# The opening of a hybrid GDN/MLA encoder block on one core: x issued ahead of the vectors, the first modulation slice in four transfers, its high part in halves on two engines, and the norm spread ahead of the first products

## The chip, the cores and the metric

The kernel runs on one core of a Trainium2 chip. The metric is the device time of one execution in microseconds, taken as the median of several runs. Engines are called as the profile calls them: PE (TensorE, its weight loads apart as PEld), DVE (VectorE), ACT (ScalarE), POOL (GpSimd) and SP (SyncE, which here issues all loads).

## The reference, cut to what matters

One layer of a streaming encoder: a macaron SwiGLU half-step, a token mixer (gated DeltaNet beside latent attention), and a second SwiGLU half-step. Each is fed by an adaptive RMSNorm whose shift, scale and gate come from one small vector `c`. The change sits almost wholly in the first of the three modulations and the first columns of the first SwiGLU product.

```python
D_MODEL = 1024; SEQ = 512; D_FF = 2816; N_MOD = 9

def _modulate(x, shift, scale):
    return _rms(x) * (1.0 + scale[:, None, :]) + shift[:, None, :]

sc = jax.nn.silu(c)
mod = sc @ w_ada[l] + b_ada[l]
sh1, s1, g1, sh2, s2, g2, sh3, s3, g3 = jnp.split(mod, N_MOD, axis=-1)
h = _modulate(x, sh1, s1)
x = x + 0.5 * g1[:, None, :] * _swiglu(h, ffn1_w_in[l], ffn1_w_out[l])
...
```

`x` is 512 tokens by 1024, `w_ada` is 1024 by 9216, `ffn1_w_in` is 1024 by 5632, all float32.

## The kernel before, in words

**Precision.** Each large product is computed from float32 operands that are split into a high part (a cast to the matmul type, on ACT) and a low part (the rest, a subtraction on DVE). `mm3` (L451 to L455) then issues three products: high by high (L453), activations' low part (L454), weights' low part (L455). So each weight tile `wr` becomes `wh` and `wl`, and each tile of the modulated activations `h` becomes `hh` and `hl`.

**The opening** is `setup` (L465) and `phase0` (L484). `setup` issues loads on SP in the order of the code: `c` and `b_ada` as 80 short rows into one tile `vecs`, then `x` as four tiles `xt` of 128 tokens (512 KB each). `phase0` then issues the columns of `w_ada` that give shift and scale of the first 128 model columns ("slice 0", two transfers `ar` of 512 KB, `phase0_slice`, L603), the first 128 rows of the SwiGLU weights for six output blocks (`wr`, 384 KB, `phase0_weights`), the same two for the second 128 columns, and then pairs of slices in eight transfers `ar` of 256 KB each (`phase0_pair`). All transfers go through one queue. Each carries one of eight DMA semaphores in turn, and a semaphore takes one transfer at a time, so SP issues transfer n only when transfer n-8 has landed.

What the engines do until the first product:

- PE transposes `vecs` (L496); ACT makes `sc` = silu(c) from it (L498) and DVE keeps the transposed biases `vT` (L500).
- ACT squares and sums each `xt` (L513); DVE turns the sums into `ve` (L781), POOL takes the power -1/2 (L209), which gives the norm's factor `ry` for each token.
- PE transposes `xt` in eight groups of four blocks (`raw`, L507) and DVE copies each group to `xT` (L508). Seven groups come first, the eighth after the first modulation.
- DVE scales the first 128 columns of x by `ry` (`xn`, L538) and makes `dg`, the factors on a diagonal (L655).
- PE multiplies `sc` with slice 0 in 16 passes (`phase0_cols`, L632), ACT copies the result out (`sg`, L635), PE folds it to two columns (`columns`, L525), DVE adds the biases in two instructions (shift L526, scale L527).
- PE transposes `xn` into one PSUM tile (L547), DVE copies that out (L549), and ACT makes the high part `hh` of the first 128 rows of h from it (L552); DVE makes `m` and the low part (L553, L554). ACT casts the first weights (L544), DVE makes their low part (L556).

**The loop** over the eight 128-row slices of h (`kt`, 0 to 7; L560 on) accumulates six PSUM tiles `pu`. At `kt` = 0 it issues the six high-by-high products (L569), then the spread of the norm's factors over all partitions (a product of `dg` with ones, L663, copied to `rb` by ACT, L571), then for every kt: at the first of six output blocks (`j` = 0) the 16 passes for slice kt+1 (`phase0_cols`), at `j` = 1 `columns` and the modulation of slice kt+1 (`modulated`, L688, L690, L677), and between these the split of the next weights (`weights`, L223 and L224). For kt+1 = 5 and 7 (`SUMMED`) the 16 passes are replaced by eight weighted sums (ACT L641 for the first, DVE L643 for seven) that a table, `STEPS`, hangs on stages kt = 2 and 3, and 4 and 5; there `columns` stands at `j` = 2.

**What sets the order.** All of `phase0` is recorded under `in_order`: each engine runs its instructions in the order in which the code issues them. PSUM tiles from `aux` come from a ring of five buffers, so each takes the place of the fifth before it and waits for that one's readers. What comes behind `phase0` is ordered by a scheduler, and is nearly the same in both kernels. In `gates` (far later, in the mixer) one small copy of `gdn_a_log` was free to move to an early place on DVE.

Of the kernel before, what the change touches and what calls it, by code (L numbers as in the profile page):

```python
# [31 lines left out]
STEPS = {2: (5, range(4)), 3: (5, range(4, 8)), 4: (7, range(4)), 5: (7, range(4, 8))}  # L32
# [60 lines left out]
class Block:  # L93
# [390 lines left out]
    def phase0(self):  # L484
# [10 lines left out]
        pv = self.aux()  # L495
        nc.tensor.transpose(pv[:, :80], self.vecs[:80, :], self.ident[:80, :80])  # L496
        self.sc = self.const([P, 8], s="sc")
        nc.scalar.activation(self.sc, pv[:, 72:80], AF.Silu)  # L498
        self.vT = self.const([P, 72], s="vT")
        nc.vector.tensor_copy(self.vT, pv[:, :72])  # L500
# [3 lines left out]
        def raw(b, j):  # L504
            pt = self.aux()
            for t in range(4):
                nc.tensor.transpose(pt[:, t * P:(t + 1) * P], self.xtok[b][:, (4 * j + t) * P:(4 * j + t + 1) * P], self.ident)  # L507
            nc.vector.tensor_copy(xall[:, 4 * j:4 * j + 4, b * P:(b + 1) * P], pt.rearrange("p (t c) -> p t c", t=4))  # L508

        tiles = [(b, j) for b in range(NB) for j in range(2)]  # L510
# [8 lines left out]
        self.c1, self.c2 = self.const([P, KT], s="sh"), self.const([P, KT], s="s1")  # L519
        self.new_h()  # L520

        def columns(kt, sg, pg, ones):
            k = slice(kt, kt + 1)
            for m in range(2):
                nc.tensor.matmul(pg[:, 256 + m:257 + m], sg[:, m * P:m * P + P], ones, start=True, stop=True)  # L525
            nc.vector.tensor_tensor(out=self.c1[:, k], in0=pg[:, 256:257], in1=self.vT[:, k], op=ALU.add)  # L526
            nc.vector.scalar_tensor_tensor(out=self.c2[:, k], in0=pg[:, 257:258], scalar=1.0, in1=self.vT[:, 8 + kt:9 + kt],  # L527
                                           op0=ALU.add, op1=ALU.add)
# [17 lines left out]
        for b in range(NB):  # L546
            nc.tensor.transpose(pt[:, b * P:(b + 1) * P], xn[:, b * P:(b + 1) * P], self.ident)  # L547
# [1669 lines left out]
```

## Time and profile before

| | us |
|---|---|
| runs shown: median (lowest to highest of 3) | 1040.31 (1040.15 to 1041.21) |
| the profiled execution, own time | 1040.34 |
| its span, first to last instruction | 1038.6 |
| PE busy in the span | 1022.6 (98%) |
| DVE busy | 752.9 (72%) |
| ACT busy | 498.3 (48%) |
| first product of the SwiGLU on PE starts at | 16.03 |
| granted PE clock | 1.000 |

The profiled execution's own time is 1.74 us over its span and 0.03 us over the median of the runs. Times in the views are microseconds from the start of the span. In a row of the timeline the first number is the start, the second the duration, "x4" counts merged instructions, and the bracket tells how long the engine had been idle and what ended that. "SPq" rows are the issue of a transfer, not its run. In the table of stretches each engine has its busy time in that stretch, then come the granted PE clock, the DMA engines' share (over 1 where packets overlap) and their rate in GB/s.

### The profile page before, as it was taken

The numbers are of one execution on the slowest core, as the hardware profiler recorded it, in microseconds if no ns is written. First come the engines' busy times: TensorE is split into PE (matmuls) and PEld (weight loads), VectorE is DVE, ScalarE is ACT, GpSimd is POOL, SyncE is SP. The second block draws the span as 40 slices with busy tenths as digits, with TensorE's granted clock in tenths as the row PEclk, the third lists the DMA queues.
The fourth block names the chain that finished last, engine by engine and source line by source line (L and its number), as shares of the span: only waits on it lengthen the run. The fifth ranks groups of instructions, "written<-read, shape, count | busy, mean of one in ns | idle before, by whom it ended". The sixth has DMA issues, their size and how long they took to land.

```text
span 1038.6 us, 16766 instructions
## 1 busy us (share of the span) xinstructions
PE 1022.6 (98%) x6601; PEld 906.7 (87%) x6601; DVE 752.9 (72%) x1327; ACT 498.3 (48%) x910; POOL 29.7 (3%) x74
## 2 busy tenths in 40 slices
PE   6999999999999999999999999999999999999998
PEld 5788899999887898888788779998999999987888
DVE  5789788887787747868787467787888888783221
ACT  4452455556322235478864455374555555631211
POOL 0000000001100000000000001100000000000000
PEclk9999999999999999999999999999999999999999
DMA  9978234244688745211232021113333334473311
GB/s 331 321 229 257 70 94 122 84 120 128 204 292 293 240 115 145 62 42 41 62 80 68 22 82 41 42 31 100 95 99 105 109 96 121 117 270 105 111 48 42
DMA packets 201501, 130.77 MB, mean 126 GB/s; under 512 B 14017, under 2 KB 186062, under 8 KB 201422
## 3 DMA queue, kind: packets, MB, share of 16 engines
q1 hardware_dynamic: 201422, 129.69, 41.0%
q8 instruction: 52, 0.85, 0.3%
q14 instruction: 27, 0.22, 0.1%
HBM read 127.18 MB, written 2.49 MB: 125 GB/s over the span
## 4 chain that ended last, share of the span: by engine, by line
PE 93%; DVE 3%; issue 2%; DMA 1%; SPq 0%; POOL 0%; ACT 0%; POOLq 0%
PE pa L453 17%; PE pa L454 17%; PE pa L455 17%; PE pa L341 17%; PE pb L341 12%; PE pb L1942 1%; PE pb L453 1%; PE pb L455 1%; PE pb L454 1%; PE pb L1922 1%; DMA ar<-in_w_ada 1%; PE pb L1537 1%; PE pb L632 1%; PE pb L1489 0%; PE pb L1924 0%
## 5 line engine op out<-in xcount | busy, mean ns | idle before, releaser
L223 ACT CAST wh<-wr 128x1024 fp32r<-128x1024 f32 (+1 forms) x104 | 103.7, 1002 | 196.4 <-PE pa L454 171.7
L224 DVE TENSOR_TENSOR wl<-wr,wh 128x1024 fp32r<-128x1024 f32 (+1 forms) x104 | 120.5, 1163 | 79.8 <-ACT wh L223 77.8
L453 PE MATMUL pa<-ah,wh 128*128 128x512 f32 (+1 forms) x396 | 146.5, 370 | 0.0
L454 PE MATMUL pa<-al,wh 128*128 128x512 f32 (+1 forms) x396 | 145.0, 366 | 0.0
L455 PE MATMUL pa<-ah,wl 128*128 128x512 f32 (+1 forms) x396 | 144.9, 366 | 0.0
L257 DVE TENSOR_TENSOR wl<-wr,wh 128x1024 fp32r<-128x1024 f32 x90 | 110.0, 1223 | 44.4 <-ACT wh L261 44.4
L453 PE MATMUL pa<-hh,wh 128*128 128x512 f32 (+1 forms) x357 | 136.9, 383 | 0.0
L455 PE MATMUL pa<-hh,wl 128*128 128x512 f32 (+1 forms) x357 | 135.4, 379 | 0.0
L454 PE MATMUL pa<-hl,wh 128*128 128x512 f32 (+1 forms) x357 | 135.3, 379 | 0.0
L261 ACT CAST wh<-wr 128x1024 fp32r<-128x1024 f32 x90 | 91.8, 1052 | 3.7 <-PE pa L454 2.7
L453 PEld LDWEIGHTS pa<-ah,wh 128*128 128x128 f32 x396 | 74.7, 189 | 14.5 <-ACT wh L223 2.5
L455 PEld LDWEIGHTS pa<-ah,wl 128*128 128x128 f32 x396 | 74.7, 189 | 12.1
L454 PEld LDWEIGHTS pa<-al,wh 128*128 128x128 f32 x396 | 74.7, 189 | 11.7
L813 DVE SCALAR_TENSOR_TENSOR aa<-ar,sc,aa 128x512 f32<-128x512 f32 x98 | 73.4, 750 | 8.1 <-DMA ar<-in_w_ada 6.2
L453 PEld LDWEIGHTS pa<-hh,wh 128*128 128x128 f32 x357 | 67.3, 189 | 13.1 <-ACT th L1264 0.8
L455 PEld LDWEIGHTS pa<-hh,wl 128*128 128x128 f32 x357 | 67.2, 188 | 11.6
L454 PEld LDWEIGHTS pa<-hl,wh 128*128 128x128 f32 x357 | 67.3, 189 | 10.8
L341 PE MATMUL pa<-hh,wh 128*128 128x256 f32 x240 | 68.0, 283 | 0.0
L341 PE MATMUL pa<-th,wh 128*128 128x256 f32 x240 | 67.9, 283 | 0.0
L341 PE MATMUL pa<-tl,wh 128*128 128x256 f32 x240 | 67.9, 283 | 0.0
L341 PE MATMUL pa<-th,wl 128*128 128x256 f32 x240 | 67.9, 283 | 0.0
L341 PE MATMUL pa<-hh,wl 128*128 128x256 f32 x240 | 67.9, 283 | 0.0
(434 smaller groups left out, 2373.1 us busy)
## 6 DMA issues: line engine op xcount, KB each, us to landing
wr<-in_ffn_w_in SPq DMA_DIRECT2D x79, 512.0 KB, 4.9
ar<-in_w_ada SPq DMA_DIRECT2D x104, 256.0 KB, 5.4
wr<-in_ffn_w_out SPq DMA_DIRECT2D x32, 512.0 KB, 4.0
wr<-in_w_in SPq DMA_DIRECT2D x21, 512.0 KB, 3.8
ar<-in_w_ada SPq DMA_DIRECT2D x20, 512.0 KB, 6.4
wr<-in_ffn_w_out SPq DMA_DIRECT2D x16, 384.0 KB, 5.1
wr<-in_w_out SPq DMA_DIRECT2D x8, 512.0 KB, 3.3
wr<-in_ffn_w_in SPq DMA_DIRECT2D x8, 384.0 KB, 5.9
```

The costliest lines, as they stand in the source:

```text
L223: self.nc.scalar.copy(hi, raw)
L224: self.nc.vector.tensor_tensor(out=lo, in0=raw, in1=hi.bitcast(F32), op=ALU.subtract)
L257: sub = lambda out, x, y: nc.vector.tensor_tensor(out=out, in0=x, in1=y, op=ALU.subtract)
L261: nc.scalar.copy(hi[:, :n], raw[:, :n])
L341: nc.tensor.matmul(z, a[:, j, :], b, start=start and j == 0 and i == 0, stop=j == 3 and i == 2, skip_group_check=not start)
L453: mm(out, wh, xh, start=start, stop=False)
L454: mm(out, wh, xl, start=False, stop=False)
L455: mm(out, wl, xh, start=False, stop=stop)
L632: nc.tensor.matmul(pg[32 * q:32 * q + 32, :256], self.sc[:, kc:kc + 1].to_broadcast([P, 32]), a[kc], start=(e == 0), stop=(e == 1), tile_p ...
L813: nc.vector.scalar_tensor_tensor(out=acc, in0=a, scalar=sc, in1=acc, op0=ALU.mult, op1=ALU.add)
L1537: nc.tensor.matmul(pa[:, ps], kh[:, ps], x[:, ps], start=True, stop=True)
L1922: nc.tensor.matmul(ps[:, :n], self.qnT[h][:, ts], self.knT[h][:, :n], start=True, stop=False)
```

## The change

It does seven things, all in the opening but the last:

1. SP issues `x` first, then `c` and `b_ada`.
2. Slice 0 is loaded in four transfers: rows 0 to 767 of `w_ada` for shift and for scale, then rows 768 to 1023 for each.
3. The transpose of `vecs`, `sc` and `vT` move behind the fifth group of x transposes and behind the squares; DVE also makes the biases once as pairs (`cb`), so that `columns` is one DVE instruction for shift and scale together (`c12`).
4. Three of the eight copies to `xT` (groups 5 to 7) go from DVE to ACT, and the eighth group's transposes move ahead of slice 0's passes.
5. `xn` is transposed into two PSUM tiles of 256 tokens. The high part of the first tile of h is made straight from them: the first half on ACT, the second on DVE. The copy to SBUF (L549) is gone.
6. The spread of the norm's factors stands ahead of the first products instead of behind them; the split of the next weights moves behind the modulation at kt = 1 and 2; the sums of slices 5 and 7 are placed by a new table (`ORDER`: before, within and after the modulation), and `columns` stands at `j` = 1 for them too.
7. In `gates` the copy of `gdn_a_log` is tied behind the first instruction there.

```diff
-STEPS = {2: (5, range(4)), 3: (5, range(4, 8)), 4: (7, range(4)), 5: (7, range(4, 8))}
+ORDER = {2: ((), (), ((5, range(3)),)), 3: (((5, range(3, 5)),), ((5, range(5, 6)),), ((5, range(6, 8)),)),
+         4: ((), (), ((7, range(3)),)), 5: (((7, range(3, 5)),), ((7, range(5, 6)),), ((7, range(6, 8)),))}
...
     def setup(self):
-        self.load(self.vecs[72:80, :], ins["c"].rearrange("o (t p) -> (o t) p", p=P))
-        self.load(self.vecs[0:72, :], ins["b_ada"].rearrange("o (t p) -> (o t) p", p=P))
         xd = ins["x"][0]
...
+        self.load(self.vecs[72:80, :], ins["c"].rearrange("o (t p) -> (o t) p", p=P))
+        self.load(self.vecs[0:72, :], ins["b_ada"].rearrange("o (t p) -> (o t) p", p=P))
...
-        for i in range(4):
-            raw(*tiles[i])
+        for i in range(5):
+            raw(i, nc.vector.tensor_copy)
         r = self.rms_cols(v, NB, D)
-        for i in (4, 5, 6):
-            raw(*tiles[i])
+        pv = self.aux()
+        nc.tensor.transpose(pv[:, :80], self.vecs[:80, :], self.ident[:80, :80])
+        nc.scalar.activation(self.sc, pv[:, 72:80], AF.Silu)
+        nc.vector.tensor_copy(self.vT, pv[:, :72])
+        nc.vector.tensor_copy(bias[:, :, 0], self.vT[:, :8])
+        nc.vector.tensor_scalar(out=bias[:, :, 1], in0=self.vT[:, 8:16], scalar1=1.0, scalar2=None, op0=ALU.add)
+        for i in range(5, 8):
+            raw(i, nc.scalar.copy)
...
-            nc.vector.tensor_tensor(out=self.c1[:, k], in0=pg[:, 256:257], in1=self.vT[:, k], op=ALU.add)
-            nc.vector.scalar_tensor_tensor(out=self.c2[:, k], in0=pg[:, 257:258], scalar=1.0, in1=self.vT[:, 8 + kt:9 + kt],
-                                           op0=ALU.add, op1=ALU.add)
+            nc.vector.tensor_tensor(out=c12[:, kt, :], in0=pg[:, 256:258], in1=bias[:, kt, :], op=ALU.add)
...
-        nc.vector.tensor_copy(t, pt)
         columns(0, *cols)
+        pr = self.spread_diag(dg, NB)
...
-        nc.scalar.activation(hh, t, AF.Identity, scale=self.c2[:, 0:1], bias=self.c1[:, 0:1])
-        nc.vector.tensor_scalar(out=m, in0=t, scalar1=self.c2[:, 0:1], scalar2=self.c1[:, 0:1], op0=ALU.mult, op1=ALU.add)
+        nc.scalar.activation(hh[:, l], pts[0], AF.Identity, scale=self.c2[:, 0:1], bias=self.c1[:, 0:1])
+        for out, pt, ts in ((hh, pts[1], u), (m, pts[0], l), (m, pts[1], u)):
+            nc.vector.tensor_scalar(out=out[:, ts], in0=pt, scalar1=self.c2[:, 0:1], scalar2=self.c1[:, 0:1],
+                                    op0=ALU.mult, op1=ALU.add)
...
     def phase0_slice(self, kt):
-        for m in range(2):
-            self.load(a[:, :, m, :], a1[:, m * D + kt * P:m * D + (kt + 1) * P].rearrange("(k p) n -> p k n", p=P))
+        for k0, k1 in ((0, 6), (6, KT)) if kt == 0 else ((0, KT),):
+            for m in range(2):
+                self.load(a[:, k0:k1, m, :], a1[k0 * P:k1 * P, m * D + kt * P:m * D + (kt + 1) * P].rearrange(
+                    "(k p) n -> p k n", p=P))
```

**SP, the first transfers.** Here stand the loads from the start of the program: `vecs` is c and b_ada, `xt` a tile of x, `ar_100` slice 0, `wr` weights, `ar_107` (then `ar_109`) slice 1. Before:

```order
L131 DMA vecs_73<-in_c 8x128
L131 DMA vecs_73<-in_b_ada 72x128
L131 DMA xt_76<-in_x 128x1024
L131 DMA xt_78<-in_x 128x1024
L131 DMA xt_80<-in_x 128x1024
L131 DMA xt_82<-in_x 128x1024
L131 DMA ar_100<-in_w_ada 128x8x128 x2
L131 DMA wr_103<-in_ffn_w_in 128x2x384
L131 DMA ar_107<-in_w_ada 128x8x128 x2
```

The same engine and place in the change:

```order
L132 DMA xt_74<-in_x 128x1024
L132 DMA xt_76<-in_x 128x1024
L132 DMA xt_78<-in_x 128x1024
L132 DMA xt_80<-in_x 128x1024
L132 DMA vecs_73<-in_c 8x128
L132 DMA vecs_73<-in_b_ada 72x128
L132 DMA ar_100<-in_w_ada 128x6x128 x2
L132 DMA ar_100<-in_w_ada 128x2x128 x2
L132 DMA wr_105<-in_ffn_w_in 128x2x384
L132 DMA ar_109<-in_w_ada 128x8x128 x2
```

The two vector loads have moved from the first two places to the fifth and sixth, and slice 0 has become four transfers; everything behind them keeps its order and its sizes.

**PE, from the last x transposes to the first products.** `pb_186` and `pb_248` before are the seventh and eighth group of x transposes, `pb_220` slice 0's passes and their fold, `pb_232` the transposed `xn`, `dg_215` the diagonal of the norm, `pa_254` the first of the six accumulators. Before:

```order
L507 MATMUL pb_186<-ident_84,xt_82 128x128 x4
L632 MATMUL pb_220<-ar_100,sc_132 32x256 x8
L547 MATMUL pb_232<-ident_84,xn_210 128x128 x4
L525 MATMUL pb_220<-sel_136,sg_229 128x1 x2
L507 MATMUL pb_248<-ident_84,xt_82 128x128 x4
L569 MATMUL pa_254<-hh_194,wh_104 128x512
...
L569 MATMUL pb_259<-hh_194,wh_104 128x512
L663 MATMUL pb_271<-dg_215,ones_89 128x512
L632 MATMUL pb_274<-ar_107,sc_132 32x256 x8
```

In the change (`pb_180` is the transposed `vecs`, `pb_186` to `pb_198` the last three groups of x, `pb_242` and `pb_243` the two halves of `xn`):

```order
L521 MATMUL pb_180<-ident_84,vecs_73 128x80
L506 MATMUL pb_186<-ident_84,xt_78 128x128 x4
L506 MATMUL pb_192<-ident_84,xt_80 128x128 x4
L506 MATMUL pb_198<-ident_84,xt_80 128x128 x4
L652 MATMUL pb_230<-ar_100,sc_136 32x256 x8
L552 MATMUL pb_242<-ident_84,xn_220 128x128 x2
L552 MATMUL pb_243<-ident_84,xn_220 128x128 x2
L532 MATMUL pb_230<-sel_132,sg_239 128x1 x2
L683 MATMUL pb_251<-dg_225,ones_89 128x512
L586 MATMUL pa_262<-hh_204,wh_106 128x512
...
L586 MATMUL pb_267<-hh_204,wh_106 128x512
L652 MATMUL pb_278<-ar_109,sc_136 32x256 x8
```

The spread (L663, now L683) has moved from behind the six products to ahead of them, the eighth group of x from behind the fold to ahead of slice 0's passes, and the transpose of `vecs` from the head of PE's program into the groups of x.

**DVE, stages kt = 2 and 3 of the loop.** `hm` is the modulated slice, `hl` its low part, `wl` the next weights' low part, `sg_394` (then `sg_395`) the sum for slice 5. Before, from the end of stage 2's modulation:

```order
L677 SCALAR_TENSOR_TENSOR hl_201<-hm_390,sh_192,hh_200 128x512
L643 SCALAR_TENSOR_TENSOR sg_394<-ar_313,sc_132,sg_394 128x256
L643 SCALAR_TENSOR_TENSOR sg_394<-ar_315,sc_132,sg_394 128x256
L643 SCALAR_TENSOR_TENSOR sg_394<-ar_317,sc_132,sg_394 128x256
L224 TENSOR_TENSOR wl_368<-wr_366,wh_367 128x768
L526 TENSOR_TENSOR sh_192<-pb_436,vT_134 128x1
L527 SCALAR_TENSOR_TENSOR s_193<-pb_436,vT_134 128x1
L688 SCALAR_TENSOR_TENSOR hm_454<-xT_98,s_193,rb_270 128x512
L643 SCALAR_TENSOR_TENSOR sg_394<-ar_319,sc_132,sg_394 128x256
L643 SCALAR_TENSOR_TENSOR sg_394<-ar_321,sc_132,sg_394 128x256
L677 SCALAR_TENSOR_TENSOR hl_203<-hm_454,sh_192,hh_202 128x512
L643 SCALAR_TENSOR_TENSOR sg_394<-ar_323,sc_132,sg_394 128x256
```

The same place in the change:

```order
L541 TENSOR_TENSOR wl_312<-wr_310,wh_311 128x768
L663 SCALAR_TENSOR_TENSOR sg_395<-ar_316,sc_136,sg_395 128x256
L663 SCALAR_TENSOR_TENSOR sg_395<-ar_318,sc_136,sg_395 128x256
L541 TENSOR_TENSOR wl_370<-wr_368,wh_369 128x768
L663 SCALAR_TENSOR_TENSOR sg_395<-ar_320,sc_136,sg_395 128x256
L663 SCALAR_TENSOR_TENSOR sg_395<-ar_322,sc_136,sg_395 128x256
L533 TENSOR_TENSOR c_135<-pb_435,cb_134 128x2
L708 SCALAR_TENSOR_TENSOR hm_455<-xT_98,c_135,rb_260 128x512
L663 SCALAR_TENSOR_TENSOR sg_395<-ar_324,sc_136,sg_395 128x256
L697 SCALAR_TENSOR_TENSOR hl_213<-hm_455,c_135,hh_212 128x512
L663 SCALAR_TENSOR_TENSOR sg_395<-ar_326,sc_136,sg_395 128x256
L663 SCALAR_TENSOR_TENSOR sg_395<-ar_328,sc_136,sg_395 128x256
```

One of the sums has moved from stage 2 into stage 3, two now stand between the weights' low part and the bias instruction, one instead of two between the modulation and its low part, and the bias instructions are one. Stages 4 and 5 change in the same way for slice 7.

More of the change, by code (lines that the diff above doesn't have):

```diff
@@ L569, in phase0 @@
                     nc.tensor.matmul(pu[j], hi[:, j, :], xh, start=True, stop=False)
[L570 to L571 removed]
+            early = ORDER.get(kt, ((), (), ()))
             for j in range(6):
                 if j == 0 and more:
[L574 to L575 removed]
                     if kt + 1 in SUMMED:
@@ L578, in phase0 @@
                     else:
+                        if kt > 2:
+                            high(kt + 1)
                         cols = self.phase0_cols(kt + 1, slices[kt + 1])
-                    if kt in (1, 2):
-                        w = weights(kt + 1)
-                if j == (2 if kt + 1 in SUMMED else 1) and more:
+                    if kt > 2:
+                        if kt + 1 in SUMMED:
+                            high(kt + 1)
+                        low(kt + 1)
+                    for e in early[0]:
+                        steps(*e)
+                if j == 1 and more:
                     columns(kt + 1, *cols)
@@ L585, in phase0 @@
                     next(made)
[L586 to L595 removed]
+                    for e in early[1]:
+                        steps(*e)
+                    drain(made)
+                    if kt < 3:
+                        high(kt + 1)
+                        low(kt + 1)
+                    for e in early[2]:
+                        steps(*e)
                 if kt > 0:
```

74 lines of the change are left out of this document (34 added, 40 removed).

## The prediction, made before the change was run

> **What bounds the kernel now.** I read the busy shares first, then the table of stretches, to see where TensorE stands still.
>
> ```profile
> PE 1022.6 (98%) x6601; PEld 906.7 (87%) x6601; DVE 752.9 (72%) x1327; ACT 498.3 (48%) x910; POOL 29.7 (3%) x74
> 0.00:3.00 3.00, 0.10 (x1) 0.12 (x1) 0.00 (x0) 1.49 (x2) 1.32 (x11) 1.00 0.29 34
> 3.00:6.00 3.00, 0.57 (x3) 0.36 (x4) 0.30 (x2) 0.50 (x2) 0.00 (x0) 1.00 0.87 325
> 6.00:10.00 4.00, 4.00 (x25) 4.00 (x24) 2.77 (x4) 3.65 (x7) 0.00 (x0) 1.00 1.05 381
> 10.00:16.00 6.00, 3.26 (x34) 2.17 (x31) 4.89 (x16) 2.54 (x5) 1.02 (x1) 1.00 1.13 359
> 16.00:24.00 8.00, 7.97 (x56) 4.92 (x56) 4.54 (x8) 2.41 (x4) 0.00 (x0) 1.00 1.09 390
> 23.04:60.00 36.96, 36.96 (x217) 28.25 (x217) 27.02 (x51) 18.76 (x30) 0.00 (x0) 1.00 0.85 284
> 60.00:1000.00 940.00, 935.96 (x6068) 835.98 (x6067) 708.45 (x1241) 463.88 (x856) 27.33 (x62) 1.00 0.40 119
> ```
>
> From 23 to 60 us TensorE has no gap, and from 60 to 1000 it has 4 us of them. So every later microsecond is TensorE's own work, and an opening that ends earlier shifts all of it. The DMA engines' share is full from 6 to 24 us at 359 to 390 GB/s: the opening is a race between one full queue and the small work that needs what it brings.
>
> Next the timeline of the opening, cut to the chain that leads to the first product, and the loads that it needs.
>
> ```profile
> 0.81 0.41 SPq L131 DMA_DIRECT2D vecs<-in_c  x1
> 1.27 0.31 SPq L131 DMA_DIRECT2D vecs<-in_b_ada  x1
> 1.63 1.78 SPq L131 DMA_DIRECT2D xt<-in_x  x4
> 2.90 0.36 PE L496 MATMUL pb<-ident,vecs 80*128 80x80 f32 x1 [2.90 <-DMA vecs<-in_b_ada]
> 3.45 2.21 SPq L131 DMA_DIRECT2D ar<-in_w_ada  x2
> 5.68 1.06 ACT L513 ACTIVATE jk<-xt 128x1024 f32<-128x1024 f32 x1 [2.19 <-DMA xt<-in_x]
> 10.65 0.17 DVE L781 TENSOR_SCALAR ve<-v 128x4 f32<-128x4 f32 x1 [0.67 <-ACT jk L513]
> 10.91 1.02 POOL L209 TENSOR_TENSOR ry<-ve,mhalf 128x4 f32<-128x4 f32 x1 [8.89 <-DVE ve L781]
> 12.53 0.87 DVE L538 TENSOR_SCALAR xn<-xt,ry 128x128 f32<-128x128 f32 x4
> 12.59 1.09 PE L632 MATMUL pb<-ar,sc 128*32 128x256 f32 x16 [2.02 <-DMA ar<-in_w_ada]
> 13.61 0.66 PE L547 MATMUL pb<-ident,xn 128*128 128x128 f32 x4
> 13.75 0.37 ACT L635 COPY sg<-pb 128x256 f32<-128x256 f32 x1 [3.13 <-PE pb L632]
> 14.02 0.84 ACT L544 CAST wh<-wr 128x768 fp32r<-128x768 f32 x1
> 14.18 0.61 PE L525 MATMUL pb<-sel,sg 128*128 128x1 f32 x4
> 14.91 0.15 DVE L526 TENSOR_TENSOR sh<-pb,vT 128x1 f32<-128x1 f32 x1
> 15.16 0.81 ACT L552 ACTIVATE hh<-hm,sh,s 128x512 fp32r<-128x512 f32 x1 [0.30 <-DVE s L527]
> 16.03 0.96 PE L569 MATMUL pa<-hh,wh 128*128 128x512 f32 x3 [0.75 <-ACT hh L552]
> ```
>
> TensorE waits 2.02 us for slice 0; from there each step starts when the one before ends, until the first product at 16.03. The norm's branch is no better: `ry` is ready at 11.93, but `xn` starts at 12.53, since DVE is copying x groups. The chain of waits, which follows the end of the program back to its causes, agrees, and prices three more steps:
>
> ```profile
> 4.15 8.30 DMA ar<-in_w_ada
> 17.68 0.86 PE pb L663 x2
> 23.11 1.02 PE pb L632 x16
> 24.14 0.43 PE pa L453
> ```
>
> Slice 0 lands at 4.15 + 8.30 = 12.45; the spread costs TensorE 0.86; slice 2's 16 passes start at 23.11, and the products of kt = 1 follow at 24.14. One more row tells when the queue has brought slice 2:
>
> ```profile
> 22.93 0.37 SPq L131 DMA_DIRECT2D ar<-in_w_ada  x1
> ```
>
> By the order of loads this is the eighth transfer behind the last one of slices 2 and 3, with the same semaphore, and SP has issued seven since; so it is that landing that lets it go, at about 22.91. In the kernel before it was harmless: the last two of the 16 passes, which alone need it, start at 23.11 + 14/16 of 1.02 = 24.00.
>
> **The change part by part.** *The queue.* x is issued at 0.81 (where `c` was) and not at 1.63: 0.82 us earlier. The 40 KB of vectors now stand in the full queue: 0.11 at 0.36 MB/us. Everything behind them keeps sizes and order, so it lands 0.71 earlier, if the queue stays full. Bounds: 0, if the queue's start-up does not move, to 0.82. I take 0.71, because x is 2 MB at the head of a queue that was filling just then (34, then 325 GB/s). Slice 0 lands at 11.74, its first three quarters at 11.74 - 0.26/0.36 = 11.0.
>
> *Slice 0's passes.* Twelve of 16 need only the first two transfers: 11.15 (a landing is followed 0.14 later, 12.45 to 12.59) to 11.9. The last four take 0.26 behind 11.88, so the passes end near 12.15; before, at 13.68.
>
> *The norm.* Four squares end 0.82 earlier; `ve` at 9.83, `ry` at 11.11. DVE has no x copies left there, only the bias preparation (three small instructions, the nearest row L526 with 0.15), so `xn` runs from 11.2 to 12.1, just before TensorE is free for it at 12.15. The two transposes of 0.66 end at 12.8.
>
> *To the first product.* `sg` 12.2 to 12.6, the fold (0.61) behind the transposes 12.75 to 13.35, one bias instruction instead of two until 13.65. For the high part on ACT no row shows a half tile from PSUM: the nearest are the 128x256 copy `sg` (0.37) and the 128x512 row of L552 (0.81). I take 0.45, nearer to the copy, which has the same size and source. Ahead of it stands the cast of the weights (0.84), which need 384 KB behind slice 0: 11.74 + 0.39/0.36 = 12.8, so 12.85 to 13.7, and the half tile ends near 14.2. DVE's half is done earlier. The spread (0.86) fills TensorE's wait from 13.35 to 14.2. First product: **14.25, 1.78 earlier**. And behind the six products 0.86 of spread is gone, so TensorE reaches slice 2's passes 2.64 earlier, at 20.47. Slice 1 lies between: 1 MB and 384 KB behind slice 0 need 4.0 us at 359 GB/s, so it lands at 15.75, and TensorE asks for it at 14.25 + 1.65 = 15.9. Just in time.
>
> *Slice 2.* Its last transfer lands at 22.91 - 0.71 = 22.2. The passes for the others run ahead; the last two start at 22.34 and not at 24.00. So of 2.64 us gained **1.0 is given back as a wait for the queue, and 1.65 stays.**
>
> *Costed at nothing, with their cover.* That 1.0 us of wait covers anything that makes the first product late by less.
>
> ```profile
> 7.71 0.69 DVE L508 COPY xT<-pb 128x512 f32<-128x512 f32 x1 [0.16 <-PE pb L507]
> 18.58 0.59 ACT L571 COPY rb<-pb 128x512 f32<-128x512 f32 x1 [2.60 <-PE pb L663]
> ```
>
> The three copies on ACT (0.59 to 0.69 each) lie between the squares' end and `sg`, 10.05 to 12.1; each 0.1 over that delays `sg` by as much. The vectors land near 9.1 (4.86 and three more tiles, then 0.11) instead of before 2.9; `sc` then waits for the fourth square on ACT (about 10.05) and is needed at 11.15; behind their transpose on PE stand three x groups, which wait with it. SP issues two transfers more, and the eight-semaphore rule now makes the quarter transfers wait for x tiles 1 and 2 (5.68 - 0.82 = 4.86, and one tile of 0.52 MB at 0.38 MB/us later, 6.2); behind them queue all further loads, but at 6.2 the queue still holds two x tiles and three quarters of slice 0, 1.8 MB or 4.9 us. The copy in `gates` moves 16 bytes a partition. The sum, made against the profiled execution's own 1040.34 (span 1038.6, 0.03 over the median): 1040.34 - 1.65 = **1038.7**.
>
> [...] The stretch at 16 to 24 us carries mostly 256 KB transfers at 390 GB/s, that at 10 to 16 mostly 512 KB ones at 359: in a full queue smaller was not slower. [...]
>
> **The rivals.** *The queue moves further than thought, and TensorE does not wait for slice 2.* Then all 2.64 stay: 1037.7. For it: the first x packets come while the queue is empty. Against it: the queue has been full since 6 us, and it would have to land 1.7 earlier with 0.8 of head start.
>
> *The queue does not move.* If filling it takes until about 4 us whatever is issued first (325 GB/s in 3 to 6), slice 2 lands at 22.91, its last passes start at 23.05: 0.95 earlier, 1039.4.
>
> *DVE becomes the bound in stages 3 and 5 (slower than the forecast, and than before if it grows).*
>
> ```profile
> 29.92 0.50 PE L453 MATMUL pa<-hh,wh 128*128 128x512 f32 x1
> 34.57 1.52 DVE L643 SCALAR_TENSOR_TENSOR sg<-ar,sc,sg 128x256 f32<-128x256 f32 x3
> 35.74 0.50 PE L453 MATMUL pa<-hh,wh 128*128 128x512 f32 x1
> 36.00 0.95 DVE L224 TENSOR_TENSOR wl<-wr,wh 128x768 fp32r<-128x768 f32 x1
> 37.46 0.75 DVE L688 SCALAR_TENSOR_TENSOR hm<-xT,s,rb 128x512 f32<-128x512 f32 x1
> 39.05 0.74 DVE L677 SCALAR_TENSOR_TENSOR hl<-hm,sh,hh 128x512 fp32r<-128x512 f32 x1
> 40.46 0.39 PE L453 MATMUL pa<-hh,wh 128*128 128x512 f32 x1
> ```
>
> Stage 3 lasts 4.72 us on TensorE (35.74 to 40.46). DVE's work in it rises to five sums (0.51 each), 0.95, 0.75, 0.74 and 0.15, in all 5.1, and the fold of slice 5 comes one block (0.69) sooner. If DVE enters the stage without slack, TensorE waits 0.4 + 0.69 = 1.1, and again in stage 5: 1040.9. It decides if DVE ends stage 2 later than TensorE; stage 2 lasts 5.8 us (29.92 to 35.74) and has by the same rows 3.6 of DVE work (0.75, 0.74, 0.95, 0.15 and two sums), so I expect slack.
>
> *The two extra transfers hold up the queue (slower than before).* The vectors' 36 KB took 1.6 us from issue (1.27) to use (2.90). If each extra transfer stopped the queue for as long, slice 2 would land 3.2 later, at 25.4, its last passes start at 25.55 and the kernel ends at 1041.9. It decides from 1.65 us of stop on. Against it: in the stretches above the share stays full over some twenty transfers. [...]
>
> **How the numbers follow.** The forecast has 0.58, with 1038.7. No wait for slice 2: 0.16 (1037.7). A queue that does not move: 0.10 (1039.4). DVE: 0.08 (1040.9). Extra transfers: 0.06 (1041.9). Else 0.02. The range 1037.3 to 1040.2 holds the first three, with half a microsecond for the unknown durations at either end, and leaves out the rest. A measurement of this kernel can tell about 0.2%, 2.1 us, from no change: faster than 1038.2 is the second case and a tenth of the first (0.22), slower than 1042.4 is half of the last rival and the rest (0.05), and 0.73 lies between.
>
> **What would show it.** Right: the first x tile used at about 4.85; slice 0's passes in two parts ending near 12.2; the first product (L586) at 14.25, within 0.5; the spread (L683) ahead of it; about 1 us of TensorE waiting for `ar` within slice 2's passes; the first product of kt = 1 near 22.5; no gap from there to 60. Wrong: no wait at slice 2's passes (second case), that wait with the old landing (third), gaps at `columns` of slices 5 and 7 (DVE), or a DMA share that drops between 9 and 13 us (transfers).

## The result and the profile after

The kernel after takes **1041.93 us** (median of 22 runs, 1041.32 to 1046.0); the kernel before, run beside it, 1040.37 (22 runs, 1039.65 to 1042.99). The ratio is 1.0017, 95% interval 1.0011 to 1.0023: 1.6 us slower, where the prediction had 1.65 us faster. Its range ended at 1040.2. The profiled execution of after took 1041.64 with a span of 1039.8, so 1.30 more than that of before.

The table of stretches first, of the kernel after, for the five stretches in which before was shown:

```profile
0.00:3.00 3.00, 0.00 (x0) 0.00 (x0) 0.16 (x1) 1.49 (x2) 1.31 (x11) 1.00 0.34 81
3.00:6.00 3.00, 1.45 (x7) 1.48 (x8) 0.32 (x1) 1.44 (x3) 0.00 (x0) 1.00 1.01 385
6.00:10.00 4.00, 3.05 (x22) 2.85 (x21) 2.95 (x5) 3.08 (x7) 0.00 (x0) 1.00 1.08 351
10.00:16.00 6.00, 5.00 (x35) 2.91 (x34) 3.25 (x15) 3.47 (x9) 1.02 (x1) 1.00 1.16 302
16.00:24.00 8.00, 7.84 (x52) 4.60 (x51) 4.81 (x8) 2.18 (x4) 0.00 (x0) 1.00 1.08 352
```

Until 6 us the queue did what was predicted: it starts earlier and fills sooner (81 and 385 GB/s, before 34 and 325). Then it falls behind: 351, 302 and 352 GB/s where before had 381, 359 and 390. The DMA engines' share stays over 1 all the while (1.08, 1.16 and 1.08). So the queue never stands empty; each byte takes the engines longer.

Next the timeline of the kernel after, TensorE's rows of the opening, with the first use of x on ACT ahead of them:

```profile
4.44 1.06 ACT L516 ACTIVATE jk<-xt 128x1024 f32<-128x1024 f32 x1 [2.15 <-DMA xt<-in_x]
11.82 1.88 PE L652 MATMUL pb<-ar,sc 128*32 128x256 f32 x16 [0.99 <-DVE xn L545]
13.64 0.66 PE L552 MATMUL pb<-ident,xn 128*128 128x128 f32 x4
14.17 0.60 PE L532 MATMUL pb<-sel,sg 128*128 128x1 f32 x4
14.64 1.11 PE L683 MATMUL pb<-dg,ones 128*128 128x512 f32 x2
15.76 0.93 PE L586 MATMUL pa<-hh,wh 128*128 128x512 f32 x3
...
17.44 1.09 PE L652 MATMUL pb<-ar,sc 128*32 128x256 f32 x16
...
21.97 2.27 PE L652 MATMUL pb<-ar,sc 128*32 128x256 f32 x14
24.99 0.62 PE L652 MATMUL pb<-ar,sc 128*32 128x256 f32 x2 [0.75 <-DMA ar<-in_w_ada]
25.54 0.50 PE L454 MATMUL pa<-hh,wh 128*128 128x512 f32 x1
```

The last three rows are slice 2's passes and the first product of kt = 1. In the kernel before they read:

```profile
23.05 1.09 PE L632 MATMUL pb<-ar,sc 128*32 128x256 f32 x16
24.07 0.50 PE L453 MATMUL pa<-hh,wh 128*128 128x512 f32 x1
```

x is used 1.24 earlier than before (5.68), but the first product starts only 0.27 earlier (16.03), and TensorE's lead of 1.08 at slice 2's passes (21.97, before 23.05) turns into a loss: 16 passes that need 1.02 take until 25.54, waiting for transfer after transfer. The first product of kt = 1 starts 1.47 later than before (24.07). That is the whole loss (1.30 in the executions' own times): from 60 us on TensorE is busy 240.00 of 240.00 us to 300 in both kernels, and then 695.89 to 1000 us here against 695.96. (The bracket at 11.82 names `xn`; but `xn` runs from 11.42 to 12.29. It was the second of slice 0's four transfers, whose last part landed at 11.69.)

Two things were read from single DMA packets and from semaphores. In the opening of before a packet of 512 B took 27 ns, one of 1024 B 46 and one of 1536 B 65, nearly always the same (7826 of 7835 packets from 8 to 26 us); in after 512 B took 32 on average in 8 to 16 us (28 to 33 from one microsecond to the next), 1024 B 51 and 1536 B 79. And the semaphore of each large transfer goes up by one sixteen times (for slice 2's last transfer in before from 22.21 to 22.91); each count is taken here for the landing of one part, on one of the sixteen DMA engines, though the trace doesn't name the engine. The table gives, for the last transfer of slice 2, when the first, the fifteenth and the last part landed, with what followed:

| run | slice 0 last | slice 2 first / 15th / last part | first product of kt = 1 | own time |
|---|---|---|---|---|
| before | 12.45 | 22.21 / 22.80 / 22.91 | 24.07 | 1040.34 |
| before again (e1) | 12.96 | 22.64 / 24.25 / 25.02 | 25.61 | 1041.83 |
| after | 12.55 | 23.34 / 24.28 / 24.95 | 25.54 | 1041.64 |
| e4, tiles at 256 B | 11.72 | 21.39 / 22.93 / 23.17 | 23.76 | 1039.61 |
| e13, e4 again | 11.88 | 21.72 / 23.43 / 23.68 | 24.27 | 1039.89 |
| e5, before at 64 B | 12.94 | 24.09 / 24.64 / 24.68 | 25.27 | 1041.29 |
| e6, after at 128 B | 12.23 | 23.41 / 23.92 / 25.44 | 26.03 | 1041.70 |

The time is the start of that product plus 1015.6 to 1016.3 us in every row: what the opening gains or loses is settled there. These are single executions, and not always typical ones: those of e4 and e5 are among the fastest of their eleven runs (e5's the very fastest), those of e7 and e10 below are the slowest of theirs.

### The profile page after: what moved, and what is told of

Read it like the earlier page. It is cut to its first block, busy times and chain, and to the rows that moved or that the text cites. A ratio compares the mean times of both kernels' runs of the same rounds, so it can differ in the third digit from the quotient of the medians.

```text
span 1039.8 us, 16774 instructions
## 1 busy us (share of the span) xinstructions
PE 1024.5 (99%) x6601; PEld 907.1 (87%) x6601; DVE 751.5 (72%) x1319; ACT 499.2 (48%) x913; POOL 29.6 (3%) x74
## 4 chain that ended last, share of the span: by engine, by line
PE 90%; DVE 3%; DMA 2%; issue 2%; ACT 1%; SPq 1%; POOL 0%; DVEq 0%; ACTq 0%; POOLq 0%
PE pa L454 17%; PE pa L455 17%; PE pa L456 17%; PE pa L342 17%; PE pb L342 12%; SPq L132 1%; PE pb L1962 1%; PE pb L454 1%; PE pb L455 1%; PE pb L456 1%; DMA wr<-in_ffn_w_in 1%; DMA ar<-in_w_ada 1%; PE pb L1942 1%; PE pb L1509 1%; ACT bd L1587 0%
## 5 line engine op out<-in xcount | busy, mean ns | idle before, releaser
L224 ACT CAST wh<-wr 128x1024 fp32r<-128x1024 f32 (+1 forms) x97 | 97.8, 1015 | 197.4 <-PE pa L455 176.0
L225 DVE TENSOR_TENSOR wl<-wr,wh 128x1024 fp32r<-128x1024 f32 (+1 forms) x97 | 113.7, 1178 | 75.9 <-ACT wh L224 74.3
```

The lines of the kernel that those rows point to most:

```text
L224: self.nc.scalar.copy(hi, raw)
L225: self.nc.vector.tensor_tensor(out=lo, in0=raw, in1=hi.bitcast(F32), op=ALU.subtract)
```

## The experiments

Ratios are to the kernel before in runs on the same chip (21 to 33 runs of it each time, medians 1040.36 to 1040.79). The sets ran on three chips (the first and the fourth on one), so times of different sets are compared by the ratios; where medians are compared across sets, the text says so.

**First set: is it the change at all, and which part of the issue order?** Both kernels with no edit, one execution each, then after with the vectors issued first, and after with slice 0 in two transfers:

```diff
 e2     def setup(self):
+        self.load(self.vecs[72:80, :], ins["c"]...)
+        self.load(self.vecs[0:72, :], ins["b_ada"]...)
         xd = ins["x"][0]
 e3     def phase0_slice(self, kt):
-        for k0, k1 in ((0, 6), (6, KT)) if kt == 0 else ((0, KT),):
+        for k0, k1 in ((0, KT),):
```

> The kernel before, unchanged, for its packets beside those of the others on one chip. Theory 1 (the change itself slows the transfers' queue): 359 GB/s from 10 to 16 us and 390 from 16 to 24, as in its first trace, first product near 16.0, products of kt = 1 from 24.1. Rival (the slow queue in the trace of the change belongs to that chip or that execution): 300 to 350 GB/s here as well, and slice 2's passes wait for the queue.

> The changed kernel, unchanged. Theory 1: 300 GB/s from 10 to 16 us and 350 from 16 to 24 once more, products of kt = 1 from 25.5. Rival (chip or execution): a rate that differs from the first trace, with first product and slice 2 moved along with it, and no fixed distance to the kernel before.

> The changed kernel with the loads of c and b_ada ahead of x, as before; all else stays. Theory 1a (the order of issue upsets the queue): the rate is back at 359 and 390 GB/s, slice 0 lands at 12.45 as before, slice 2 at 22.9 and kt = 1 starts 0.95 earlier than before: about 1039.4, 2.5 us faster than the changed kernel. Theory 1b (the four transfers upset the queue): rates stay at 300 and 350, the time at about 1041.9.

> The changed kernel with slice 0 in two transfers of 512 KB, x still first. Theory 1a (the order of issue upsets the queue): rates stay at 300 and 350 GB/s, the time at about 1041.9 or a little more, since all of slice 0's passes wait for its end. Theory 1b (the four transfers upset the queue): rates of 359 and 390, slice 2 lands 0.7 earlier than before, about 1038.7.

The stretch from 10 to 16 us of each, in this order:

```profile
10.00:16.00 6.00, 3.32 (x32) 2.27 (x32) 4.68 (x16) 2.59 (x5) 1.02 (x1) 1.00 1.11 331
```
```profile
10.00:16.00 6.00, 6.00 (x39) 4.22 (x38) 2.75 (x14) 3.90 (x9) 1.03 (x1) 1.00 1.14 305
```
```profile
10.00:16.00 6.00, 4.63 (x33) 2.51 (x31) 3.19 (x16) 3.60 (x9) 1.02 (x1) 1.00 1.15 305
```
```profile
10.00:16.00 6.00, 4.17 (x39) 2.97 (x39) 2.67 (x15) 3.52 (x9) 1.02 (x1) 1.00 1.15 305
```

Three kernels with the change have the same 305 GB/s and packets of 32 and 51 ns on average; before has 27 and 46 ns again, so the longer packets belong to the change and not to the chip. The second run of after took 1042.28 us. And neither edit undid it: e2 1042.81 us, ratio 1.0026 (1.0017 to 1.0035); e3 1041.97, 1.0015 (1.0006 to 1.0023). Both theories on the issue order fell. The second profile of before told something else: nearly all its packets are as short as ever, and yet it moved 331 GB/s and took 1041.83 us, 1.5 more than in the first. Four packets from 14 to 16 us took 0.84 to 1.42 us each. The parts of slice 1's first transfer landed within 1.2 us, those of its second, at that time, within 2.7, and slice 2's last part landed at 25.02. The trace doesn't say which engine had which packet, so that these four delayed those parts is an inference.

**Second set: where the tiles lie.** What remained was something that all kernels with the change share. In the built program of before the SBUF tiles that the opening's loads go to start at a multiple of 256 B in their partition (`ar` of slice 0 at 203776, the first `wr` at 56320); in after each starts 64 B past one (203840, 56384). The cause is in the diff, in words that look like bookkeeping: two small constants of 32 B in a partition (`sh`, `s1`) became two of 64 B (`cb`, `c12`), and everything behind them moved by 64 B. So: the same two kernels, instruction for instruction, with one small constant widened.

```diff
-        self.sel4 = self.const([P, 1], s="sel4")
+        self.sel4 = self.const([P, 49], s="sel4")[:, :1]    (e4, after: 192 B more, tiles back at 256 B)
+        self.sel4 = self.const([P, 17], s="sel4")[:, :1]    (e5, before: 64 B more; e6, after: at 128 B)
```

> The kernel after, instruction for instruction the same, with the small tile sel4 widened from 1 to 49 columns: 192 B more per partition, so that every later SBUF tile (the x tiles, the slices, the weight tiles, the slots) starts at a multiple of 256 B again, as in the kernel before; in the kernel after they start 64 B past one. Theory 2 (the place of the destinations in SBUF slows the queue): packets of 512 and 1024 B back at 27 and 46 ns (after: 31 to 34 and 51), the core's transfers back near 359 GB/s in 10 to 16 us and 390 in 16 to 24 (after: 302 and 352), first product for k-tile 1 at 22.4 to 23.2 us (after: 25.54), median 1038.3 to 1039.3 us. Rival (the slower queue comes from the order or the number of what is issued, in a way that neither vectors first nor two transfers undid): 302 and 352 GB/s and 1041.9 us, as after.

> The kernel before, instruction for instruction the same, with sel4 widened from 1 to 17 columns: 64 B more per partition, so that every later SBUF tile starts 64 B past a multiple of 256 B, as in the kernel after, and nothing else of the change. Theory 2: packets at 31 to 34 and 51 ns, about 302 GB/s in 10 to 16 us and 350 in 16 to 24; the 5.27 MB that before moves from 10 to 24 us then take some 16 us, so slice 2 lands 1.5 to 2.3 us later and the median is 1041.8 to 1042.8 us. Rival: 27 and 46 ns, 359 and 390 GB/s, 1040.4 us.

> The kernel after with sel4 widened to 17 columns: every later SBUF tile starts 128 B past a multiple of 256 B. [...] Theory 2 with steps of 128 B: as on a multiple of 256 B, 27 and 46 ns, 359 and 390 GB/s, 1038.3 to 1039.3 us. If places do not matter: 1041.9 us, and the run on a multiple of 256 B gives that as well.

The stretches 10 to 16 and 16 to 24 us of e4, then of e5, then of e6:

```profile
10.00:16.00 6.00, 5.35 (x36) 3.22 (x35) 3.85 (x16) 3.55 (x7) 1.02 (x1) 1.00 1.12 347
16.00:24.00 8.00, 7.63 (x52) 4.19 (x51) 4.02 (x6) 1.95 (x4) 0.00 (x0) 1.00 1.08 383
```
```profile
10.00:16.00 6.00, 3.82 (x36) 2.74 (x34) 4.69 (x16) 1.97 (x5) 1.02 (x1) 1.00 1.15 305
16.00:24.00 8.00, 7.48 (x49) 4.77 (x52) 4.23 (x9) 2.87 (x5) 0.00 (x0) 1.00 1.10 345
```
```profile
10.00:16.00 6.00, 5.99 (x40) 3.80 (x39) 3.38 (x15) 3.87 (x7) 1.02 (x1) 1.00 1.17 305
16.00:24.00 8.00, 7.14 (x49) 4.25 (x47) 4.49 (x7) 1.87 (x4) 0.00 (x0) 1.00 1.10 352
```

The same instructions have packets of two lengths, and the place of the tiles chooses which. e4 has packets of 27 and 46 ns; e5 and e6 have 32 to 33 and 51 on average. The packet's length is the surer sign: the rate in GB/s also falls when single packets take very long, as in the second profile of before (331 from 10 to 16 us) and in e7 below (303), both with packets of 27 ns. Medians: e5 1043.01, ratio 1.0024 (1.0015 to 1.0033): 64 B of padding alone make the kernel before at least as slow as the change did (1041.8 to 1042.8 was expected). e6 1041.70, 1.0009 (0.9999 to 1.0019): 128 B off costs the packets what 64 B off costs (32 to 33 and 51 ns in both), so Theory 2 with steps of 128 B fell, though its time alone would not tell it from e4's. e4 1040.88 (1039.32 to 1042.02), 1.0001 (0.9992 to 1.0010): the loss against before is gone. But the gain of 1.65 is not there either, and e4 missed what was expected of it (1038.3 to 1039.3); that took two more sets.

That the place does it is shown; how it does it is not. 1536 B packets took longer too, some 76 ns in e5 and e6 against 65 in before, but 4096 B packets, and packets in the emptier queue from 60 us on, took no longer (see the last section).

**Third set: what sets the time once the rate is back?** In e4, TensorE's rows around slice 2 (those of before stand above):

```profile
21.04 1.88 PE L652 MATMUL pb<-ar,sc 128*32 128x256 f32 x14
23.21 0.62 PE L652 MATMUL pb<-ar,sc 128*32 128x256 f32 x2 [0.30 <-DMA ar<-in_w_ada]
23.76 0.50 PE L454 MATMUL pa<-hh,wh 128*128 128x512 f32 x1
```

TensorE is 2.01 us ahead of before at the passes (21.04 against 23.05) and has 0.31 left behind them: it still waits for slice 2, whose last part landed at 23.17. So in e7 (on e4) and e8 (on after) these passes stand two output blocks later, and two more undo one part each of the change, where nothing hides it any longer.

```diff
+            late = 2 if kt == 1 else 0
             for j in range(6):
-                if j == 0 and more:
+                if j == late and more:
...
-                if j == 1 and more:
+                if j == late + 1 and more:
                     columns(kt + 1, *cols)
```

> The kernel after with its tiles at multiples of 256 B (as e4) and one more edit: in k-tile 1 TensorE does slice 2's passes and their column sums two products groups (6 products, 2.06 us) later, so that it goes on with k-tile 1's products in place of waiting for slice 2. Theory A (in the kernel after, and still in e4, the landing of slice 2's last transfer sets the time, and TensorE's lead from the earlier stages is given back there): the first product for k-tile 1 moves from 23.76 us in e4 to about 21.1, the passes then take 1.1 us without a wait, and some 1.3 to 1.7 us are kept: median 1038.9 to 1039.7 us (e4 1040.88). Rival (TensorE isn't what is late there; what follows k-tile 1 waits for something else, such as slice 4 or the modulation, which starts 2 us later): within 0.4 us of e4, 1040.5 to 1041.3 us.

> The kernel after as it is (tiles 64 B past multiples of 256 B) with slice 2's passes two groups of products later, as in e7. Theory A: the wait that the slow queue makes at slice 2 (passes 21.97 to 25.54 us, 2.5 us more than their 1.02) is covered for 2.06 us; what is left is up to 0.5 us there and the later landing of slice 0 (0.7 us against e4), so 1039.6 to 1040.6 us, within 1.2 us of e7, and the packets stay at 33 and 51 ns. Rival: 1041.5 to 1042.3 us, as after.

> e7 with the norm's spread and its copy put back behind k-tile 0's first six products, as in the kernel before: the one term of the prediction that moved work (0.86 us). Prediction's account (the spread lies in a wait for the first products when it is ahead of them, and TensorE's lead counts once nothing waits at slice 2): 0.5 to 0.9 us slower than e7. Rival (the first products then start earlier by nearly as much, since the high part in halves is ready by then): within 0.2 us of e7.

> e7 with slice 0 in two transfers, as in the kernel before: prices the four transfers where no landing of slice 2 hides them. Prediction's account: passes of slice 0 that start when all has landed end some 0.7 us after the landing more (1.09 us of passes, of which 0.41 stay behind the last landing with four transfers): 0.5 to 0.8 us slower than e7. Rival (what follows the passes waits for xn or the weights' high part, not for the passes): within 0.2 us of e7.

| run | median (lowest to highest of 11) | ratio (95%) |
|---|---|---|
| e7 | 1039.33 (1038.67 to 1040.34) | 0.9985 (0.9977 to 0.9994) |
| e8 | 1040.30 (1040.12 to 1041.80) | 0.9996 (0.9987 to 1.0005) |
| e9 | 1039.80 (1039.38 to 1040.54) | 0.9986 (0.9977 to 0.9995) |
| e10 | 1039.24 (1038.79 to 1040.62) | 0.9986 (0.9977 to 0.9995) |

Theory A holds: covering the wait is worth 1.6 us (e7 to e4, by the medians and by the ratios, whose intervals overlap by 0.0002), as predicted, and with the slow queue as much or more (e8 to after, 1.6 by the medians and 2.2 by the ratios, whose intervals lie apart). In the profiled execution of e7 slice 0 landed late (12.51), so that the products of kt = 1 start at 22.76 and not at 21.1; but the passes run without a wait, though slice 2's last part landed only at 24.89. Its passes, then the products of kt = 1 in e8, which run on until the passes, two groups later:

```profile
24.87 1.09 PE L653 MATMUL pb<-ar,sc 128*32 128x256 f32 x16
```
```profile
21.78 0.50 PE L454 MATMUL pa<-hh,wh 128*128 128x512 f32 x1 [0.17 <-ACT wh L537]
22.12 0.40 PE L455 MATMUL pa<-hl,wh 128*128 128x512 f32 x1
22.77 0.50 PE L456 MATMUL pa<-hh,wl 128*128 128x512 f32 x1 [0.26 <-DVE wl L541]
```

Of the two parts, the spread behaves as predicted in the trace of e9. The rows show the wait that it otherwise fills, and slice 1's passes 0.84 later than in e4 (16.49):

```profile
14.92 0.93 PE L583 MATMUL pa<-hh,wh 128*128 128x512 f32 x3 [0.98 <-ACT hh L557]
15.69 0.85 PE L583 MATMUL pb<-hh,wh 128*128 128x512 f32 x3
16.38 1.02 PE L683 MATMUL pb<-dg,ones 128*128 128x512 f32 x2
17.33 1.09 PE L652 MATMUL pb<-ar,sc 128*32 128x256 f32 x16
```

In the time it is 0.47 by the medians and not told from nothing by the ratios (0.9986 and 0.9985). The four transfers are worth nothing that can be measured (e10 is 0.09 under e7), where 0.5 to 0.8 was expected.

**Fourth set: why four transfers gain nothing, what x first is worth, and the late part.**

```diff
 e11    def phase0_cols(self, kt, a):
-        for q in range(4):
-            for e in range(2):
-                kc = 2 * q + e
+        for e in range(2):
+            for q in range(4):
+                kc = q + 4 * e
```

> e7 with the passes dealt to TensorE's four column groups the other way: group q takes rows q and q+4 of the slice's eight, not 2q and 2q+1 (the sums over the eight are the same sums in another order). Theory B (why four transfers were worth nothing in e10): in e4 the last four records of slice 0's 16 passes, all of one column group, start 0.21 us apart (11.86, 12.08, 12.29, 12.51) where 16 over four groups start 0.05 apart, so the quarter that lands last costs 1.03 us, as much as all 16 (1.09) after a single landing. With the last quarter in two groups its two pairs overlap: passes of slice 0 end 0.43 us earlier after the landing, first product 0.3 to 0.45 earlier, median 1038.8 to 1039.1 us (e7 1039.33). Rival (xn or the weights' cast is what the first product waits for): 1039.2 to 1039.5.

> e7 with c and b_ada issued ahead of x, as in the kernel before: prices the earlier issue of x (0.82 us) where neither the slow queue nor the wait at slice 2 hides it. Prediction's account: all landings 0.71 us later, first product 0.6 to 0.8 later, median 1039.9 to 1040.2 us (e7 1039.33). Rival (the queue's start sets the landings whatever is issued first, or the vectors that land late behind x cost as much as x gains): within 0.2 us of e7.

> e4's kernel again, for a second profile. In e4 single packets took up to 1.4 us from 14 to 16 us, their DMA engines stayed behind the others by that much, and slice 2's last sixteenth landed at 23.17 where the other engines had brought theirs by 22.4. Theory C (this belongs to the execution and not to the kernel): other engines or none fall behind this time, slice 2 lands between 22.2 and 23.5 accordingly, and the time goes with it (1038.7 to 1039.1 us without a late engine, 1040 and more with one later than e4's). Rival (it belongs to the kernel's order of transfers): the same delay at the same place and 1039.3 to 1039.8 us.

First e4, slice 0's passes and what follows them; then e11:

```profile
11.14 1.75 PE L652 MATMUL pb<-ar,sc 128*32 128x256 f32 x16 [0.64 <-DMA ar<-in_w_ada]
12.82 0.66 PE L552 MATMUL pb<-ident,xn 128*128 128x128 f32 x4
...
14.93 0.94 PE L586 MATMUL pa<-hh,wh 128*128 128x512 f32 x3
```
```profile
11.20 1.42 PE L653 MATMUL pb<-ar,sc 128*32 128x256 f32 x16
12.55 0.66 PE L552 MATMUL pb<-ident,xn 128*128 128x128 f32 x4
...
14.67 0.94 PE L586 MATMUL pa<-hh,wh 128*128 128x512 f32 x3
```

From slice 0's landing to the transposes of `xn`, which follow the passes, e4 needs 1.10 us (11.72 to 12.82) and e11 0.69 (11.86 to 12.55): 0.41 less, where 0.43 was expected. e10, with slice 0 in two transfers, needs 1.16 (12.32 to 13.48): four transfers dealt as in e4 save 0.06. In e4 the last four records start at 11.86, 12.08, 12.29 and 12.51; in e11 at 11.99, 12.00, 12.21 and 12.24, two side by side. Theory B holds in the traces. The median is **1038.67** (1038.14 to 1039.78), ratio 0.9979 (0.9970 to 0.9988): this version is faster than both kernels, 0.2% under before. From e7 it differs by 0.0006, less than the intervals tell apart, so the 0.41 is not shown in the time.

e12 takes 1039.96 us, 0.9993 (0.9984 to 1.0002): 0.63 over e7 by the medians and 0.8 by the ratios, about what the prediction gave the earlier issue of x (0.71). The two intervals overlap (e7's ends at 0.9994), so this isn't told from nothing either. In its profile slice 0 lands at 12.84 and the first product starts at 16.05, where e4 has 11.72 and 14.93; a part of that is one late part, since the fifteenth part of slice 0 had landed at 12.27.

e13 took 1039.89. Its slow packets are others than e4's (above their usual duration 0.36 us in all from 14 to 15, 0.55 from 16 to 17 and 0.65 from 17 to 18, where e4 had 3.7 us from 14 to 16), its slice 2 landed 0.5 later and its time is 0.28 longer. So size and place of the slow packets go with the execution. But parts were late in this run too, as in every profile but two: the gap from the first to the last part of slice 2 was 0.70 in the first profile of before and 0.59 in e5, and 1.5 to 3.3 us in the other fourteen. Neither theory holds alone. That slow packets held up slice 2's last part is an inference in e4 too: which engine had which packet is not in the trace, and the fifteenth part landed at 22.93. What makes the slow packets stays open; a likely second cause of late parts, which comes too late to matter in those two profiles, stands in the last section.

## Why the prediction was wrong, point by point

- **The step that failed** is "Everything behind them keeps sizes and order, so it lands 0.71 earlier, if the queue stays full." It stayed full and kept sizes and order, and its rate fell all the same, by 8% from 6 to 10 us and by 10 to 16% from there on, since the change's two small constants moved every tile that is loaded by 64 B. Slice 2's first part landed at 23.34 (22.21 before) and its last at 24.95, where the forecast had 22.2; 0.67 of that is the last part alone, which the last section puts down to something else. The prediction read the diff for what it makes the engines do, not for what it does to addresses; its "queue" rivals were about issue and start-up, and no rival had the rate itself change. Shown by e4, e5 and e6: same instructions, other places. In e5, where nothing but the place changed, slice 2's last part landed 1.77 later than in before (24.68). In time, the place is worth 1.0 us by the medians and 1.7 by the ratios (e4 to after) of the 3.2 by which the forecast was missed.
- **That slice 2's landing sets the end** was right, and costlier than thought: 1.0 us was to be given back there, and the lead of 1.08 was lost with 1.47 on top. Shown by e7 and e8.
- **x first** came out as forecast in four of six profiles with x first and the tiles at 256 B: the first part of slice 2 landed at 21.39 to 21.72 in e4, e9, e11 and e13, against 22.21 before (0.71 earlier forecast, 0.49 to 0.82 measured), and slice 0 at 11.71 to 11.88 (11.74 forecast). In e7 and e10, with 13 and 12 slow packets, that part came at 22.17 and 22.16, hardly earlier than before. e12 puts the price at 0.63 by the medians, within the noise.
- **"The last four take 0.26"** was wrong. It took a quarter of the time of 16 passes that overlap over four column groups (in before each record lasts 378 ns and the starts are 0.05 us apart); the last quarter lies in one group and its records follow each other every 0.21 to 0.22 us, 1.03 us in all. Passes that were to end near 12.15 in a queue with before's rate end at 12.89 in e4, and the first product starts at 14.93 and not at 14.25. Shown by the traces of e10 and e11. In e4 itself this cost nothing at the end: TensorE was at slice 2's passes at 21.04, 2.13 ahead of the last landing, so the wait covered it, as the prediction had said of anything late by less than that wait.
- **The landing of a transfer** was taken from the mean rate and from one profile, in which the sixteen parts landed within 0.7 us. The slowest of the sixteen parts counts: in e9 fifteen parts had landed at 22.18, just where the forecast had the whole, and the last at 23.11. The second profile of before shows that it has such executions too. In e4's profiled execution the last part at 23.17 moved the first product of kt = 1 from the forecast 22.5 to 23.76, and it took 1039.61 and not 1038.7. Its eleven runs fall into two groups, 1039.32 to 1039.79 and 1040.88 to 1042.02, and the median is the lowest of the second; no trace of that group was kept, so that its loss comes from late landings too is likely but not shown.
- **The spread ahead** (0.86) fills the wait as forecast; e9's trace has it (0.84), its time only in part. The half tile on ACT took 0.56 (L558, forecast 0.45).
- **The rivals.** No gap at `columns` of slices 5 and 7: all of TensorE's 0.75 us of idle time from 24 to 60 us in after lie ahead of 24.99. Small transfers: the two last pieces of slice 0, 128 KB each, landed 0.35 and 0.37 behind what stood ahead of them in e4, the queue's full rate (128 KB in 0.36 us is 364 GB/s). The rival of extra transfers named the right time, 1041.9, by the wrong cause, which is luck: e3 has two transfers less and the same time. The prediction also took a difference under 2.1 us for one that can't be told from none; with 22 runs of each kernel the interval is 1.2 us wide, and the 1.6 us of loss are clear of it. And its range reaches 0.4 us below and 0.8 above the cases that it holds, not half a microsecond at either end.

## What to carry to other kernels

Before pricing a change, compare the addresses of what the DMA writes: two small constants that grew by 32 B each, allocated ahead of the large tiles, cost this kernel 1.0 to 1.7 us (after, by medians and by ratios) and 2.6 us (the same shift in before), against 1.65 that the change was meant to gain, and 192 B of padding undo it. Ask of a wait for a transfer whether work behind it could go first (e7: three lines, 1.6 us), and expect a landing at its slowest part, not its mean (23.11 against 22.18 for the fifteenth in e9). Ask of a load cut in pieces whether the work on the last piece still fills the engine: here four transfers saved 0.06 us behind the landing with the last four passes in one column group (e4) and 0.41 more with them in two (e11), and that 0.41 is not seen in the time.

## What the runs showed of the hardware that was not expected

- Packets to SBUF tiles that start 64 or 128 B past a multiple of 256 B took mostly 33 on average instead of 27 ns (512 B) and 51 instead of 46 (1024 B) while the queue was full, in all seven profiles of such kernels; at a multiple of 256 B nearly all took 27 and 46, in all nine. The queue moved 302 to 306 GB/s from 10 to 16 us and 345 to 352 from 16 to 24 in those seven. In the nine it moved 347 to 359 and 381 to 390 where few packets were slow (the first profile of before, e4, e9, e13) and 303 to 337 and 352 to 384 in the other five. Packets of 4096 B (x) showed no such difference (159 ns in both at the median), and from 60 us on, below 300 GB/s, the median for 512 B was 27 ns in both kernels (means 28.5 and 28.7), though nearly all tiles of after lie 64 B off there as well.
- Single packets of 512 to 1536 B took 0.3 to 2 us in many executions, most often from 14 to 17 us. From 8 to 26 us there were 0, 1, 3, 4, 6, 10, 12, 13 and 13 of over 0.3 us in the nine profiles with tiles at a multiple of 256 B, and 0, 0, 0, 0, 1, 2 and 5 in the seven with tiles off it. No run tests whether the place of the tiles has to do with that; if it has, it takes back a part of what the shorter packets gain.
- A 16 KB packet of the instruction queue took 0.88 to 1.15 us. In after it ran from 22.17 to 23.32, ahead of slice 2's last transfer, whose last part landed 0.67 behind the fifteenth. In e2, e6 and e8, which had no packet of over 0.3 us, the last part was 0.04 to 0.09 behind the fifteenth in one transfer and 1.36 to 1.53 behind in the next, with this packet in between. In the first profile of before and in e5 it came at 23.88 and 24.82, behind slice 2's last transfer, and the same jump (0.98 and 1.13) stands two transfers later, where it harmed nothing at slice 2. In these six traces the jump comes with the packet, so it may be what holds up one part of what is loaded beside it, and in every profile of a kernel with the change it came ahead of slice 2's last landing. Its engine is not in the trace, and no run took it away, so its price in the time is not shown.
